# A rule for where the matmuls of two recurrences may enter a stream of projection matmuls

## The chip, the cores and the metric

The kernel runs on one core of a Trainium2 chip. The metric is the device time of one execution in microseconds (us), and the median of three runs before the change is 1229.77 us. TensorE runs the matmuls, VectorE (DVE) and ScalarE (ACT) the elementwise work, and SyncE (SP) issues most of the transfers.

## What is computed

One layer of a sequence model with 272 tokens (16 learned ones and 256 of the input) of width 2048. The tokens are normalised and multiplied by one wide weight matrix; its columns are the inputs of three recurrent mixers A, B and C, each with an output of width 1024. Each mixer's output is multiplied by a matrix of its own, gated and added, and a last matrix and a norm give the result.

```python
xn = rmsnorm(h, norm_g[l])
(a_q, a_f, a_i, a_z, b_q, ..., c_r, c_k, c_v, ..., g_a, g_b, g_c) = split_cols(xn @ w_in[l])
y_a = hgrn2_mixer(a_q, a_f, a_i, a_z, ...)      # A: 8 heads
y_b = mlstm_mixer(b_q, b_k, b_v, b_o, ...)      # B: 4 heads
y_c = rwkv7_mixer(c_r, c_k, c_v, c_wd, ...)     # C: 16 heads
merged = (sigmoid(g_a) * (y_a @ w_br[l, 0]) + sigmoid(g_b) * (y_b @ w_br[l, 1])
          + sigmoid(g_c) * (y_c @ w_br[l, 2]))
h = h + merged @ w_out[l]
```

Mixer A works in chunks: scores inside the chunk, weights from decays, a sum over values, a norm per head. Mixer B is a gated attention with a norm. Mixer C needs, for each chunk of 64 tokens, the inverse of a triangular matrix and then a chain of small products from chunk to chunk.

## The kernel before, in words

**The stream.** The big product is cut into projections of 256 columns (47 of them before the gates). One projection is `gemm` (line 390): four weight blocks `u` of four 128-row tiles, and for each block two column halves `j`. Weights and activations are split into a high and a low part of type fp32r, so each tile takes three matmuls; `unit` (line 377) issues the 12 matmuls of one half of a block, into the PSUM tile `gp`. A whole block is thus 24 matmuls. `Stream` brings the weights: `load` (line 343) issues the transfer on SyncE's queue, `cut` (line 351) makes `wh` on ScalarE and `wl` on VectorE, and `next` (line 367) keeps three cut blocks. A cut is emitted at the start of a block, for the block two further on.

**The recurrences.** `c_scan` (line 506), `b_scan` (line 965), `tail` of B's gates (line 875) and `a_scan` (line 1138) are Python generators that issue a few instructions and then yield. A yield of `"pe"` says that the next step begins with matmuls; another yield says that it doesn't. A scan starts with a priority: 0 for C, 1 for B, 2 for A. The four scans of A are called a0 to a3 here; each works on two heads and goes through these TensorE groups in turn: a first small group of 104 score matmuls (`aW`, `aQb`), a second small group of 72 (`aW`), a group of scores over longer distances (`aQR`), the transposes of the values (`aV`), the products with the values (`ATT`), and the column sum for the norm (`aYL`, `aYH`). B's heads go through `nM`, `bV` (twice), `bQ`, `bW` and the column sum `bHL`.

**The order.** The order of the program is made in Python by the class `Order` (line 44). It keeps a planned clock for TensorE, ScalarE and VectorE, adds an estimated cost for each instruction that is issued, and keeps for each scan the planned time at which its last result is ready. `pump` (line 87) goes over the scans in order of priority and lets each go on while its planned time is at most some distance ahead of TensorE's planned clock: 3.5 us for a step without matmuls, 0.3 us (2.0 us for C) for one with matmuls. `gemm` calls `pump` after each half of a block, so after 12 and after 24 matmuls. `finish` (line 105) issues all that is left of a scan at once; it is called where a later block needs the scan to be over. For A's scans that is behind the last projection of a group (until `ast["free"]` is set, line 1112) and behind the second projection of the next group (all of it, line 1122). Behind the program stands a scheduler that may still move an instruction that it holds to be unready behind later ones of its engine.

**Buffers.** The work tiles of A and B come from one set of six buffers (tag `wx`), and their PSUM banks from a pool of two (`bank`). C has sets of its own (`wc`, `cbank`).

Of the kernel before, what the change touches and what calls it, by code (L numbers as in the profile page):

```python
# [43 lines left out]
class Order:  # L44
# [39 lines left out]
            self.scans.remove(s)  # L84
        s["ready"], self.ready = self.ready, saved

    def pump(self):
        for e in ("act", "dve"):
            self.clk[e] = min(self.clk[e], self.clk["pe"] + self.CAP)
        moved = True  # L90
        while moved:
            moved = False
            for s in list(self.scans):
                while not s["done"]:
                    if s["hold"] is not None and not s["hold"]():
                        break
                    ahead = self.AHEAD
                    if s["pe"]:
                        ahead = self.AHEAD_PE if s["prio"] else self.AHEAD_PE_FIRST
                    if s["ready"] > self.clk["pe"] + ahead:  # L100
                        break
                    self.step(s)
                    moved = True
# [47 lines left out]
def kernel(  # L151
# [29 lines left out]
    od = Order()  # L181
# [195 lines left out]
    def unit(h, l, u, kts, ps, aH, aL, t0, n, js):  # L377
        for k in range(UK):
            kk = u * UK + k
            rh = aH[:, kk, t0:t0 + n]  # L380
            mm(ps, h[:, k, js], rh, start=kk == 0, stop=False)
            mm(ps, h[:, k, js], aL[:, kk, t0:t0 + n], start=False, stop=False)
            mm(ps, l[:, k, js], rh, start=False, stop=kk == kts - 1)

    def apart(f):
        saved, od.ready = od.ready, od.clk["pe"]
        f()
        od.ready = saved

    def gemm(m, aH, aL, kts, t0, n, evac):  # L390
        nt = m // P
        ps = [gps.tile([P, 512], F32, name="gp", tag="g") for _ in range(nt)]
        for u in range(kts // UK):
            h, l = ws.next()
            for j in range(nt):
                unit(h, l, u, kts, ps[j][:, 0:n], aH, aL, t0, n, slice(j * P, (j + 1) * P))
                od.pump()
        for j in range(nt):
            apart(lambda: evac(j, ps[j][:, 0:n]))

# [2 lines left out]
    def proj(c0, m, t0, evac, before=None, after=None):  # L403
        ws_src = win[:, :, c0:c0 + m]
        blocks.append((ws_src, KT, lambda: gemm(m, xH, xL, KT, t0, T - t0, evac), before, after))
# [1324 lines left out]
```

## Time and profile before

| | |
|---|---|
| Median of three runs | 1229.77 us (1229.72 to 1230.2) |
| The profiled execution: time | 1229.33 us |
| The profiled execution: span from the first to the last instruction | 1227.6 us |
| Mean granted TensorE clock | 0.998 |
| TensorE busy, VectorE busy, ScalarE busy | 98%, 72%, 54% of the span |

The time of an execution is its span and 1.7 us that lie around it. The profile comes from one execution, and its own time is 0.4 us below the median. A busy TensorE is not TensorE at its peak: its matmuls overlap, so the distance from one start to the next says more than the length of one.

### The profile page before, as it was taken

What the parts mean: (1) busy time and instruction counts of PE and PEld (TensorE: products, weight loads), DVE (VectorE), ACT (ScalarE), POOL (GpSimd) and SP (SyncE); (2) the same over time, 40 slices, a digit from 0 to 9 for tenths busy, and PEclk for the clock granted to TensorE, in tenths of its full rate; (3) what the DMA queues carried; (4) which work ended last, traced back from release to release, by engine and by line L of the source; (5) the groups of instructions that cost most, each with busy time, mean ns of one, the idle gap of its engine ahead of it and who ended that gap; (6) DMA issues with size and microseconds to landing.
All of it is one profiled execution on the core that took longest, in us unless ns stands there. A gap on an engine that the chain in (4) does not pass through costs nothing.

```text
span 1227.6 us, 23061 instructions
## 1 busy us (share of the span) xinstructions
PE 1208.1 (98%) x9224; PEld 1104.2 (90%) x9224; DVE 879.2 (72%) x1491; ACT 665.0 (54%) x1032; POOL 57.0 (5%) x167
## 2 busy tenths in 40 slices
PE   8999999999999999999999999999999999999997
PEld 8999999999999999999999988888888888888887
DVE  6688996697975889995889986644555565556554
ACT  6765455663445764766664657544444444445444
POOL 3100001000051000010000000000000000000000
PEclk9999999999999999999999999999999999999999
DMA  8645564465563554463554454666766676665663
GB/s 254 184 138 166 155 172 130 129 183 155 155 171 104 158 165 137 140 170 105 162 163 142 139 164 153 190 188 189 226 197 193 191 225 200 191 193 172 193 197 121
DMA packets 172996, 207.43 MB, mean 169 GB/s; under 512 B 22331, under 2 KB 127160, under 8 KB 172488
## 3 DMA queue, kind: packets, MB, share of 16 engines
q1 hardware_dynamic: 171688, 202.21, 56.2%
q0 software_dynamic: 880, 3.22, 0.8%
q8 instruction: 72, 1.18, 0.4%
q10 hardware_dynamic: 320, 0.53, 0.1%
q14 instruction: 36, 0.29, 0.1%
HBM read 202.19 MB, written 3.74 MB: 168 GB/s over the span
## 4 chain that ended last, share of the span: by engine, by line
PE 85%; DVE 9%; ACT 3%; issue 2%; POOL 0%; DVEq 0%; ACTq 0%; POOLq 0%
PE gp L186 76%; PE cbank L186 5%; DVE wl L127 3%; PE bank L186 3%; ACT wh L127 1%; DVE Ltmp L127 1%; PE cbank L193 1%; DVE LV L127 1%; PE bank L193 1%; DVE UV L127 0%; DVE aY L127 0%; ACT L127 0%; DVE BK L127 0%; DVE aW L127 0%; DVE SC L127 0%
## 5 line engine op out<-in xcount | busy, mean ns | idle before, releaser
L127 DVE TENSOR_TENSOR wl<-raw,wh 128x1024 fp32r<-128x1024 f32 (+1 forms) x370 | 449.3, 1215 | 243.6 <-ACT wh L127 242.2
L127 ACT CAST wh<-raw 128x1024 fp32r<-128x1024 f32 (+1 forms) x370 | 386.7, 1046 | 387.0 <-PE gp L186 352.4
L186 PE MATMUL gp<-xH,wh 128*128 128x272 f32 (+3 forms) x1552 | 448.1, 289 | 0.2 <-ACT xH L127 0.2
L186 PE MATMUL gp<-xH,wl 128*128 128x272 f32 (+3 forms) x1552 | 444.0, 286 | 1.6 <-DVE wl L127 1.6
L186 PE MATMUL gp<-xL,wh 128*128 128x272 f32 (+3 forms) x1552 | 443.8, 286 | 0.1
L186 PEld LDWEIGHTS gp<-xH,wl 128*128 128x128 f32 x1552 | 292.4, 188 | 2.9 <-DVE wl L127 2.6
L186 PEld LDWEIGHTS gp<-xH,wh 128*128 128x128 f32 x1552 | 292.5, 188 | 2.2 <-ACT xH L127 0.5
L186 PEld LDWEIGHTS gp<-xL,wh 128*128 128x128 f32 x1552 | 292.2, 188 | 0.9 <-DVE xL L127 0.3
L186 PE MATMUL gp<-wh,xH 128*128 128x512 f32 x384 | 150.6, 392 | 0.0
L186 PE MATMUL gp<-wh,xL 128*128 128x512 f32 x384 | 150.5, 392 | 0.0
L186 PE MATMUL gp<-wl,xH 128*128 128x512 f32 x384 | 150.3, 391 | 0.0
L186 PEld LDWEIGHTS gp<-wh,xL 128*128 128x128 f32 x384 | 72.1, 188 | 15.5
L186 PEld LDWEIGHTS gp<-wl,xH 128*128 128x128 f32 x384 | 72.2, 188 | 15.0
L186 PEld LDWEIGHTS gp<-wh,xH 128*128 128x128 f32 x384 | 72.1, 188 | 15.0
L186 PE MATMUL gp<-wh,mH 128*128 128x512 f32 (+1 forms) x144 | 51.1, 355 | 0.0
L186 PE MATMUL gp<-wh,mL 128*128 128x512 f32 (+1 forms) x144 | 50.9, 354 | 0.0
L186 PE MATMUL gp<-wl,mH 128*128 128x512 f32 (+1 forms) x144 | 50.9, 354 | 0.0
L127 DVE TENSOR_TENSOR LV<-LV,Ltmp 40x31 f32<-40x31 f32 (+15 forms) x124 | 41.0, 331 | 2.6
L127 DVE TENSOR_TENSOR Ltmp<-LU,LV 40x31 f32<-40x31 f32 (+15 forms) x124 | 41.1, 332 | 2.4
L186 PEld LDWEIGHTS gp<-wh,mL 128*128 128x128 f32 x144 | 27.2, 189 | 3.8
L186 PEld LDWEIGHTS gp<-wh,mH 128*128 128x128 f32 x144 | 27.2, 189 | 3.7
L186 PEld LDWEIGHTS gp<-wl,mH 128*128 128x128 f32 x144 | 27.2, 189 | 3.7
(420 smaller groups left out, 1476.0 us busy)
## 6 DMA issues: line engine op xcount, KB each, us to landing
raw<-in_w_in_dram SPq DMA_DIRECT2D x288, 512.0 KB, 3.7
raw<-in_w_br_dram SPq DMA_DIRECT2D x48, 512.0 KB, 4.2
raw<-in_w_out_dram SPq DMA_DIRECT2D x32, 512.0 KB, 3.6
hres<-in_x_dram POOLq DMA_DIRECT2D x2, 1024.0 KB, 5.9
xt<-in_x_dram SPq DMA_DIRECT2D x3, 512.0 KB, 5.0
raw<-in_w_in_dram SPq DMA_DIRECT2D x4, 256.0 KB
fg<-in_final_norm_g_dram POOLq DMA_DIRECT2D x1, 1024.0 KB, 5.1
scr<-SC SPq DMA_DIRECT2D x16, 40.0 KB, 1.7
```

What stands on the lines that cost most here:

```text
L127: r = f(*a, **k)
L186: nc.tensor.matmul(o, lhsT, rhs, start=start, stop=stop)
L193: nc.tensor.transpose(o, a, i)
```

## The change

`pump` gets an argument. Where it is false, a step that begins with matmuls, of a scan with a priority other than 0, is not let in. `gemm` passes false behind the first half of a weight block and true behind the second. The steps of A and B that begin with matmuls are therefore emitted behind whole blocks only, 24 matmuls apart instead of 12. C's steps, and the steps without matmuls of all three, are emitted as before, and so is everything in the later products, where `pump` is called without an argument. No instruction is added or taken away; only the order changes, and with it the planned clocks.

```diff
-    def pump(self):
+    def pump(self, whole=True):
+
         for e in ("act", "dve"):
             self.clk[e] = min(self.clk[e], self.clk["pe"] + self.CAP)
         moved = True
...
             for s in list(self.scans):
                 while not s["done"]:
                     if s["hold"] is not None and not s["hold"]():
+                        break
+                    if s["pe"] and s["prio"] and not whole:
                         break
                     ahead = self.AHEAD
...
             for j in range(nt):
                 unit(h, l, u, kts, ps[j][:, 0:n], aH, aL, t0, n, slice(j * P, (j + 1) * P))
-                od.pump()
+                od.pump(j == nt - 1)
```

## Rows read from the trace of the kernel before

**Rows 1.** The page: engines' busy time, VectorE's share and TensorE's clock in 40 slices.

```profile
PE 1208.1 (98%) x9224; PEld 1104.2 (90%) x9224; DVE 879.2 (72%) x1491; ACT 665.0 (54%) x1032; POOL 57.0 (5%) x167
...
DVE  6688996697975889995889986644555565556554
...
PEclk9999999999999999999999999999999999999999
```

**Rows 2.** The page: the chain that ended last, shares of the span by engine.

```profile
PE 85%; DVE 9%; ACT 3%; issue 2%; POOL 0%; DVEq 0%; ACTq 0%; POOLq 0%
```

**Rows 3.** Waits of TensorE: us in total, times, longest us.

```profile
PE bank L186 <- DVE aW L127: 1.6, 2, 1.0
PE gp L186 <- DVE wl L127: 1.6, 4, 0.7
...
PE bank L186 <- DVE aYL L127: 1.1, 2, 0.8
```

**Rows 4.** Timeline of TensorE (start us, us, instructions): first and last group behind half a block.

```profile
97.99 0.34 PE L193 MATMUL bank<-ident,gg 4*128 4x4 f32 x3
...
651.18 0.81 PE L186 MATMUL bank<-aW 128*32 128x32 f32 x67
```

**Rows 5.** Timeline of TensorE: a B group behind half a block, and the stream after.

```profile
186.81 0.97 PE L186 MATMUL bank<-bW,onesR 128*128 128x256 f32 x6
187.62 1.95 PE L186 MATMUL bank<-bW,bvt 128*128 128x256 f32 x12
189.42 0.36 PE L186 MATMUL gp<-xH,wh 128*128 128x258 f32 x1
```

**Rows 6.** Timeline of TensorE: the same group of another head, behind a whole block.

```profile
144.94 0.97 PE L186 MATMUL bank<-bW,onesR 128*128 128x256 f32 x6
...
147.56 0.37 PE L186 MATMUL gp<-xH,wh 128*128 128x272 f32 x1
```

**Rows 7.** Timelines of VectorE and TensorE: a last operand of B and its matmuls.

```profile
154.09 0.41 DVE L127 TENSOR_TENSOR bHL<-bSQ,bHL 128x256 fp32r<-128x256 f32 x1
...
158.23 0.40 PE L186 MATMUL bank<-bHL,onesR 128*128 128x256 f32 x2
```

**Rows 8.** Timeline of TensorE: the two small groups of a0 (in brackets: idle before, releaser).

```profile
473.43 0.81 PE L186 MATMUL bank<-aW 128*32 128x32 f32 x67
...
474.59 0.38 PE L186 MATMUL gp<-xH,wh 128*128 128x256 f32 x1
...
476.08 0.29 PE L186 MATMUL gp<-xH,wh 128*128 128x272 f32 x1
...
478.07 0.95 PE L186 MATMUL bank<-aW 128*32 128x32 f32 x72 [0.95 <-DVE aW L127]
```

**Rows 9.** Timeline of VectorE: a0's work between its two small groups.

```profile
474.95 0.43 DVE L127 TENSOR_TENSOR aW<-aE,aK 128x272 f32<-128x272 f32 x1
...
477.58 0.43 DVE L127 TENSOR_TENSOR aW<-aE,aQ 128x272 f32<-128x272 f32 x1
```

**Rows 10.** Timeline of TensorE: the end of a0.

```profile
499.74 0.82 PE L193 MATMUL bank<-ident,aV 128*128 128x128 f32 x6
...
503.53 0.37 PE L186 MATMUL gp<-xH,wh 128*128 128x256 f32 x1
...
506.89 0.36 PE L186 MATMUL bank<-aYL,onesR 128*128 128x256 f32 x1 [0.31 <-DVE aYL L127]
```

**Rows 11.** Timeline of VectorE: the last operand of that column sum.

```profile
506.07 0.68 DVE L127 TENSOR_TENSOR aYL<-aY,aYH 128x512 fp32r<-128x512 f32 x1
```

**Rows 12.** Stretches (length, busy us of each engine): while a0 and a2 run.

```profile
462.00:510.00 48.00, 46.74 (x553) 45.61 (x552) 46.37 (x109) 26.98 (x48) 0.32 (x2) 1.00 0.50 144
510.00:530.00 20.00, 19.35 (x158) 18.95 (x156) 19.79 (x43) 13.73 (x21) 0.00 (x0) 1.00 0.57 150
640.00:690.00 50.00, 48.52 (x570) 47.57 (x569) 46.94 (x109) 27.98 (x51) 0.13 (x1) 1.00 0.52 149
```

**Rows 13.** Timeline of VectorE: a1's work behind its first small group.

```profile
530.85 0.44 DVE L127 TENSOR_TENSOR aW<-aE,aK 128x272 f32<-128x272 f32 x1 [0.45 <-PE bank L186]
```

## Prediction

> **What bounds the kernel.** I read the page first. TensorE is busy for 98% of the span at full clock from end to end, and VectorE is uneven: nearly full in some slices, half idle in the last third [rows 1]. The chain that ended last is 85% TensorE and 9% VectorE [rows 2]. So time is won or lost only where TensorE stands or where its instructions lie further apart, and the second reading is the list of its waits. Most are short. Those that the change can touch directly are A's: 1.6 us in two waits for `aW`, 1.1 us in two for `aYL`, and with them 1.6 us in four waits of the stream itself for `wl`, the half of the weights that VectorE makes [rows 3]. They sum to 4.3 us, 0.35% of the time, and that bounds what a better order of A could bring.
>
> The third reading was the order of TensorE's matmuls around each group of A and B, counted in twelves of the stream. Of 44 places where such matmuls enter during the projections, 22 lie behind the first half of a block; the first is the group of B's gates at 97.99 us, the last a2's first small group at 651.18 us [rows 4]. Sixteen of these are B's and six A's. Those 22 have to move; the others already stand behind whole blocks, or were put a few matmuls further by the scheduler.
>
> **Does a place cost anything in itself?** The same B group, 18 matmuls, takes from 186.81 to 189.42 us behind half a block, 2.61 us, and from 144.94 to 147.56 us behind a whole one, 2.62 us [rows 5, 6]. So the move itself costs and gains 0: the matmuls are the same and the stream restarts alike. What is left is lateness: a moved group comes 12 matmuls later. In a0's projection these take from 474.59 to 476.08 us, 1.49 us [rows 8].
>
> **B's sixteen moves: 0.** B's operands are ready early. The tightest kind of step is the column sum: its operand ends at 154.50 us and its matmuls start at 158.23 us, 3.7 us later [rows 7]. B's order is set by the planned clock, not by data, and a delay of 1.49 us for each step leaves room before the next head's `finish`, or makes that `finish` issue elementwise work that TensorE needs only a block later. Cover: three cut weight blocks. Without it a B step could stand for at most the 1.49 us that it is late; that no wait for an operand of B is in the list at all speaks for 0. I take 0, with ends 0 and +1.5 us for one such miss.
>
> **A's first small group (a0 and a2 move; a1 and a3 already stand behind whole blocks): 0.** In a0 it runs at 473.43 us, and VectorE's next `aW` follows at 474.95 us; the last `aW` ends at 478.01 us and the second small group starts at 478.07 us after 0.95 us of standing [rows 8, 9]. VectorE's `aW` needs the buffers that the first group frees. So the chain first group, `aW`, second group is really a chain, and the move shifts it by up to 1.49 us. Does TensorE stand longer? The second group comes out of `finish`, and it stands a few matmuls inside the next block (which begins at 476.08 us), so the scheduler placed it by its own idea of when `aW` is ready. If the place goes along with the chain, the wait stays as it is; if the place stays, 1.49 us are added, twice (a0, a2), +3.0 us; if the place goes a whole half further, both waits vanish, -1.6 us [rows 3]. The place was made from the same chain, so I take 0 and keep -1.6 and +3.0 us.
>
> **A's later groups: +0.7 us.** Of a0, `aQR` and `aV` (499.74 us) stand behind halves and move. `ATT` comes one block after `aV` and ends where the stream goes on, at 503.53 us; the operand of the column sum `aYL` ends at 506.75 us, 3.2 us later, and TensorE stands 0.31 us for it behind the last matmul of that projection, where `finish` puts it [rows 10, 11]. With `aV` half a block later `ATT` can no longer be ready behind the third block and goes behind the fourth, the same place at which `finish` issues the column sum. Then nothing of the stream lies between them by program order, and what lies between them in the end is the scheduler's choice. If it puts enough of the stream between, the wait is 0: -0.3 us. If it puts nothing, 3.2 us instead of 0.31 us: +2.9 us. For a2, whose second group also comes later, the ends are -0.8 and +2.4 us. The scheduler's misses in the four A waits lie between 0.3 and 1.0 us [rows 3], so I take a miss near the upper end for both, 0.9 us against 0.31 and 0.81 us: +0.6 and +0.1 us, together +0.7 us (ends -1.1 and +5.3).
>
> **The stream's waits for `wl`: 0.** VectorE is busy for 46.4 of 48 us from 462 us, for 19.8 of the next 20, and for 46.9 of 50 us from 640 us [rows 12]. There it is close to being the bound, and four `wl` come late. What A no longer asks of VectorE at one moment, C's triangular inverse fills, and the sum of the work up to 530 us stays. A full engine finishes its queue at the same time in another order, unless it is made to stand. Bounds: all four waits gone, -1.6 us; or one half block more in each of the two stretches, +3.0 us. I take 0.
>
> In one place the trace shows VectorE standing for TensorE: 0.45 us before a1's `aW`, released by the first small group [rows 13]. By the Trainium skill ("TensorE: Matmul & The Clock Gate", section on the array of 32×32 sub-arrays) ScalarE and VectorE take their instructions strictly in order, so whatever waits at the head holds all behind it. Were that the whole story, the sum would be the rival below that holds VectorE's queue instead of 0.
>
> C's matmuls stay as they are, transfers keep their order on SyncE's queue (A and B issue none in the scans), GpSimd's few fills follow the same events.
>
> **Sum.** 0 + 0 + 0.7 + 0 = +0.7 us on the profiled execution of 1229.33 us (span 1227.6 us and 1.7 us around it) gives 1230.0 us; it lay 0.44 us below the median, so I forecast 1230.4 us for the median. What can be told from no change is about 0.2%, 2.5 us: the forecast is no measurable difference.
>
> **Rivals.**
> *Slower: the column sum stands right behind `ATT`.* As above, without the stream between: +2.9 us in a0 and +2.4 us in a2, 1235.1 us with both, 1232 to 1233 us with one or with half of each. It decides from the point at which fewer than about 12 stream matmuls lie between the two in both places. For it: `finish` issues them back to back. Against it: the scheduler has moved unready groups before, and a1's same groups show no wait.
> *Slower: VectorE's queue is held.* If `aW` of a0 and a2 stands at the head of VectorE's queue until the moved first group is done, VectorE stands up to 1.49 us in each, and as it is full until 530 us the next `wl` are as much later: +3.0 us, 1232.8 us. Against it: in a0 no such standing is seen today, since a `wl` and C's work lie in between; for it: the 0.45 us of a1 [rows 13].
> *Faster: A's waits dissolve.* If the later emission makes the scheduler put more of the stream ahead of the second small groups and the column sums, 2.7 us go; with the `wl` waits 4.3 us: 1225.5 to 1227.1 us. For it: these waits exist because the scheduler thought the operands ready too early. Against it: nothing in the change tells it better.
> *The change does not do what it says.* The scheduler behind the program may again put groups of A and B inside blocks, as it did twice with a0's and a2's second groups. Then the time is that of before, 1229.8 us.
>
> **Numbers.** The forecast gets 0.43, the rival without effect 0.10, the first slower one 0.20, the held queue 0.07, the faster one 0.20. Faster by over 0.2%: 0.20; within 0.2%: 0.53; slower: 0.27. The range leaves out the outer halves of the end cases: 1226.3 to 1234.2 us; the forecast's own range is 1228.2 to 1232.2 us.
>
> **What would show it.** Right: TensorE's groups of A and B only behind 24 matmuls (or further in, where `finish` issued them), each of the 18-matmul B groups still at 2.6 us, no new wait for an operand of B, a0's first small group near 474.7 us, `ATT` of a0 right behind the fourth block and the waits for `aYL` at most about 1 us each, waits for `wl` near 1.6 us in sum. Wrong: a wait for `aYL` or `aW` of 2 us or more; gaps of VectorE before `aW` released by TensorE's `bank`; waits of C's groups (`SC`, `UV`, `cX`) that grow although C was not touched, since the planned clocks that A and B advance are shared with it; or a total of A's and `wl`'s waits well under 2 us.

## The result, and the profile after

The changed kernel takes 1241.04 us (median of four runs, 1238.83 to 1241.42) against 1229.74 us (four runs, 1228.15 to 1230.20): a ratio of 1.0090, 95% interval 1.0073 to 1.0108. It is slower by 11.3 us, and the forecast of 1230.4 us, with its range up to 1234.2 us, is wrong. The profiled execution took 1240.92 us, its span is 1239.2 us and its mean granted clock 0.993, so 11.6 us of span are to be found. All lines have moved by three: the helper of the matmuls is L189 now, that of the transposes L196, that of the elementwise work L130.

The page of the changed kernel: engines, VectorE's share and TensorE's clock in 40 slices, and the chain by engine; these answer [rows 1, 2].

```profile
PE 1213.2 (98%) x9224; PEld 1108.1 (89%) x9224; DVE 877.8 (71%) x1491; ACT 665.3 (54%) x1032; POOL 50.4 (4%) x167
...
DVE  7687996697976889985879984744555565555554
...
PEclk9999999999999999999999998999999999999999
...
PE 83%; DVE 10%; ACT 3%; issue 2%; DMA 0%; SPq 0%; POOL 0%; DVEq 0%; ACTq 0%; POOLq 0%
```

The counts are the same. TensorE is idle for 26.0 us (1239.2 less 1213.2) against 19.5 us, and busy for 5.1 us more with the same matmuls; one slice of the clock, 743 to 774 us, has lost a tenth. Three stretches at half clock make up nearly all of these 5.1 us (last section).

Waits of TensorE in the changed kernel (us in total, times, longest us), against [rows 3]:

```profile
PE gp L189 <- DVE wl L130: 3.6, 3, 2.4
...
PE bank L189 <- DVE aQ L130: 1.5, 1, 1.5
PE bank L189 <- DVE aYL L130: 1.3, 2, 0.8
PE cbank L189 <- DVE cSL L130: 1.3, 1, 1.3
...
PE cbank L189 <- ACT UV L130: 1.1, 2, 1.0
...
PE bank L189 <- DVE aW L130: 1.1, 2, 0.6
PE cbank L189 <- ACT ZT L130: 1.1, 1, 1.1
```

The waits for `aW` and `aYL` have hardly changed. `wl` has one of 2.35 us, `aQ`, an operand of a2, has a new one, and `cSL`, `UV`, `ZT` are operands of mixer C, which the change doesn't touch. The best guide to the place is the start of the same matmul of the stream in both traces, worked out from the two timelines (after less before). The points are chosen where both kernels have issued equally many matmuls of the recurrences; only at 753.97 us has the changed kernel already issued 16 more of them:

| at (us, before) | 15 | 600 | 690 | 710 | 753.97: first product on mixer B's output | 1220 |
|---|---|---|---|---|---|---|
| later by (us) | -0.8 | -0.5 | +1.5 | +4.1 | +11.8 | +11.6 |

So the time goes at two places: 4.6 us between 600 and 710 us, ahead of the gates, and 7.7 us between 710 us and the first product on `yHB`, the high half of B's output. At the first place lie the wait for `aQ` and the long one for `wl`, which ends at 705.70 us, and the clock falls behind both (timeline of TensorE, after):

```profile
669.71 0.65 PE L189 MATMUL bank<-aQ,aK 128*64 128x64 f32 x8 [1.47 <-DVE aQ L130]
```

The second place lies between the product with the first 512 gate columns and the first product on `yHB`. There the changed kernel's TensorE does this (timeline):

```profile
755.08 0.40 PE L189 MATMUL gp<-wh,xL 128*128 128x512 f32 x1
755.57 0.45 PE L189 MATMUL cbank<-UV,BT 128*64 128x64 f32 x8
...
758.00 0.93 PE L189 MATMUL bank<-ATT,avt 128*128 128x256 f32 x4
...
761.37 0.29 PE L189 MATMUL cbank<-SC,UV 128*64 128x16 f32 x4 [0.97 <-ACT UV L130]
...
762.81 0.36 PE L189 MATMUL bank<-aYL,onesR 128*128 128x256 f32 x1 [0.79 <-DVE aYL L130]
...
764.78 0.55 PE L189 MATMUL cbank<-cSL,bonesR 128*128 128x256 f32 x1 [1.26 <-DVE cSL L130]
...
765.77 0.63 PE L189 MATMUL gp<-wh,yHB 128*128 128x512 f32 x1
766.20 0.63 PE L189 MATMUL gp<-wl,yHB 128*128 128x512 f32 x1
```

For 10.7 us the stream stands, and only the leftovers of C's last scan (`cbank`) and of a3 (`bank`) run. TensorE is busy for 7.33 us of them, the end of it at half clock, so less than 10.7 us is lost. In the kernel before the same groups of C lie between matmuls of the gate, and cost no waiting (its timeline):

```profile
741.15 0.39 PE L186 MATMUL gp<-wh,xL 128*128 128x512 f32 x1
741.47 0.45 PE L186 MATMUL cbank<-UV,BT 128*64 128x64 f32 x8
...
742.31 0.50 PE L186 MATMUL gp<-wh,xH 128*128 128x512 f32 x1
```

What ties the product to C can be read from the program and one row. `yHB` and `yLB` are allocated in `l_setup`'s pool, which takes the memory of C's pool when C's last scan is over, and ScalarE makes `yHB`. Before, and then after (tile `yHB`: ns shortest, median, longest; first and last start):

```profile
L127 ACT CAST yHB<-yB x4: 619/646/659, 746.9 to 756.5; 128x512 fp32r<-128x512 f32 x4
```

```profile
L130 ACT CAST yHB<-yB x4: 602/606/616, 764.3 to 767.7; 128x512 fp32r<-128x512 f32 x4
```

In both it follows the last small product of C's chain, which starts at 746.5 and at 761.7 us. Before it comes 0.4 us behind that, after 2.6 us, for there ScalarE first makes a last copy of C, C's squares and the gate. That chain waits for C's triangular inverse, 31 steps on VectorE, the last of which starts at 701.8 us before and at 719.1 us after (tile `LV`, before and after):

```profile
L127 DVE TENSOR_TENSOR LV<-LV,Ltmp x124: 171/350/419, 130.7 to 701.8; 40x31 f32<-40x31 f32 x8, 40x60 f32<-40x60 f32 x8, 40x87 f32<-40x87 f32 x8, 40x112 f32<-40x112 f32 x8
```

```profile
L130 DVE TENSOR_TENSOR LV<-LV,Ltmp x124: 174/350/418, 129.0 to 719.1; 40x31 f32<-40x31 f32 x8, 40x60 f32<-40x60 f32 x8, 40x87 f32<-40x87 f32 x8, 40x112 f32<-40x112 f32 x8
```

Why is the inverse 17 us late? The planner's own positions, in projections emitted before the step, name two causes. `second cV` is the step with the second transposes of C's values, the last one with matmuls ahead of the inverse; a2's `finish` stands behind 43 projections and issues a2 up to the point where its inputs are free:

```
             a1's tail ends   second cV   inverse: first step .. end
before           38.25         42.625        42.75  .. 45.75
after            38.75         43.125        43.125 .. 46.875
```

a1's later groups put its tail into the start of C's last scan (which begins behind projection 38): in the traces the first column sum of that scan runs at 601.3 us before and 603.7 us after, its scores `RA,BK` at 626.7 and 632.2 us. On the planned clock the step `second cV` went in at 736.3 us before; now it is planned ready at 749.0 us, and at the last look of `pump` ahead of a2's `finish` TensorE's planned clock is at 745.0 us: 4.0 us ahead, where 2.0 us are allowed. So the inverse is emitted behind what `finish` issues, and VectorE comes to it later: its fourth step of 31 starts at 644.3 us before and at 669.5 us after. This is theory 1. Its rivals were theory 2, that A's own late groups and the `wl` waits between 640 and 712 us are the cost, and theory 3, that B's sixteen moves are.

### The profile page after: what moved, and what is told of

Same layout as the page of the kernel before. It is cut to its first block, busy times and chain, and to the rows that moved or that the text cites. A ratio compares the mean times of both kernels' runs of the same rounds, so it can differ in the third digit from the quotient of the medians.

```text
span 1239.2 us, 23066 instructions
## 1 busy us (share of the span) xinstructions
PE 1213.2 (98%) x9224; PEld 1108.1 (89%) x9224; DVE 877.8 (71%) x1491; ACT 665.3 (54%) x1032; POOL 50.4 (4%) x167
## 4 chain that ended last, share of the span: by engine, by line
PE 83%; DVE 10%; ACT 3%; issue 2%; DMA 0%; SPq 0%; POOL 0%; DVEq 0%; ACTq 0%; POOLq 0%
PE gp L189 75%; PE cbank L189 5%; DVE wl L130 3%; PE bank L189 2%; ACT wh L130 1%; DVE Ltmp L130 1%; PE cbank L196 1%; DVE LV L130 1%; PE bank L196 1%; DVE UV L130 0%; DVE aE L130 0%; DVE aW L130 0%; DVE aM L130 0%; DVE BK L130 0%; DMA scv<-LV 0%
## 5 line engine op out<-in xcount | busy, mean ns | idle before, releaser
L130 DVE TENSOR_TENSOR wl<-raw,wh 128x1024 fp32r<-128x1024 f32 (+1 forms) x370 | 449.3, 1215 | 249.8 <-ACT wh L130 248.3
L130 ACT CAST wh<-raw 128x1024 fp32r<-128x1024 f32 (+1 forms) x370 | 386.4, 1046 | 401.4 <-PE gp L189 372.7
L189 PE MATMUL gp<-xH,wh 128*128 128x272 f32 (+3 forms) x1552 | 449.4, 290 | 0.2 <-ACT xH L130 0.2
L189 PE MATMUL gp<-xH,wl 128*128 128x272 f32 (+3 forms) x1552 | 445.5, 287 | 3.7 <-DVE wl L130 3.6
L189 PE MATMUL gp<-xL,wh 128*128 128x272 f32 (+3 forms) x1552 | 443.6, 286 | 0.1
L189 PEld LDWEIGHTS gp<-xH,wl 128*128 128x128 f32 x1552 | 293.7, 189 | 5.0 <-DVE wl L130 4.6
L189 PEld LDWEIGHTS gp<-xH,wh 128*128 128x128 f32 x1552 | 293.9, 189 | 2.6 <-ACT xH L130 0.5
L189 PEld LDWEIGHTS gp<-xL,wh 128*128 128x128 f32 x1552 | 293.6, 189 | 0.6 <-DVE xL L130 0.3
L189 PE MATMUL gp<-wh,xH 128*128 128x512 f32 x384 | 150.9, 393 | 0.0
L189 PE MATMUL gp<-wh,xL 128*128 128x512 f32 x384 | 150.3, 391 | 0.0
L189 PE MATMUL gp<-wl,xH 128*128 128x512 f32 x384 | 150.0, 390 | 0.0
L189 PEld LDWEIGHTS gp<-wh,xL 128*128 128x128 f32 x384 | 72.1, 188 | 15.7
L189 PEld LDWEIGHTS gp<-wh,xH 128*128 128x128 f32 x384 | 72.1, 188 | 15.1
L189 PEld LDWEIGHTS gp<-wl,xH 128*128 128x128 f32 x384 | 72.2, 188 | 15.0
L189 PE MATMUL gp<-wh,mH 128*128 128x512 f32 (+1 forms) x144 | 51.1, 355 | 0.0
L189 PE MATMUL gp<-wh,mL 128*128 128x512 f32 (+1 forms) x144 | 50.9, 354 | 0.0
L189 PE MATMUL gp<-wl,mH 128*128 128x512 f32 (+1 forms) x144 | 50.9, 354 | 0.0
L130 DVE TENSOR_TENSOR LV<-LV,Ltmp 40x31 f32<-40x31 f32 (+15 forms) x124 | 41.0, 331 | 2.5
L130 DVE TENSOR_TENSOR Ltmp<-LU,LV 40x31 f32<-40x31 f32 (+15 forms) x124 | 41.0, 331 | 2.4
L189 PEld LDWEIGHTS gp<-wh,mL 128*128 128x128 f32 x144 | 27.2, 189 | 3.8
L189 PEld LDWEIGHTS gp<-wh,mH 128*128 128x128 f32 x144 | 27.2, 189 | 3.7
L189 PEld LDWEIGHTS gp<-wl,mH 128*128 128x128 f32 x144 | 27.2, 189 | 3.7
```

Of the source, the lines that this page charges most:

```text
L130: r = f(*a, **k)
L189: nc.tensor.matmul(o, lhsT, rhs, start=start, stop=stop)
```

## The experiments

Times are medians; each ratio is to the kernel before in the same comparison (1229.2 to 1229.4 us in all of them).

**Whose groups?** The rule for B alone, for A alone, for all but a1, for a1 alone:

```diff
-                    if s["pe"] and s["prio"] and not whole:
+                    if s["pe"] and s["prio"] == 1 and not whole:                  # B alone; == 2: A alone
+                    if s["pe"] and s["prio"] and not whole and not s.get("free"): # all but a1
+                    if s["pe"] and s["prio"] and not whole and s.get("held"):     # a1 alone
...
             ast["scan"] = od.start(a_scan(g, st), 2)
+            ast["scan"]["free"] = g in (1,)      # or ["held"]
```

> The rule holds for B's scans alone; A's groups may enter behind halves as before. Theory 1 (a1's later tail puts off C's last scan, whose end the first gate product needs): a1's tail is where it was and C's last scan is planned to go into its triangular inverse ahead of a2's finish, as before, so 1229.8 us, 1228.5 to 1232, and the first matmul on yB starts within 2 us of the kernel before. Theory 2 (A's own late groups and the wl waits between 640 and 712 us cost it): 1229.8 us too. Theory 3 (B's sixteen moved groups cost it): 1236 us or more.

1228.99 us, ratio 0.9994 (0.9984 to 1.0004). Theory 3 falls.

> The rule holds for A's scans alone. Theory 1: C's last scan is again planned into its inverse only behind a2's finish, so nearly the whole loss, 1238 to 1241 us, with the first matmul on yB 9 us or more later than in the kernel before. Theory 2: the same time, but the loss lies ahead of the gates. Theory 3: 1230 us.

1238.93 us, 1.0084 (1.0067 to 1.0101). The stream stands for 10.7 us ahead of the first product, from 756.67 to 767.37 us, as in the changed kernel.

> The rule holds for B and for a0, a2 and a3, not for a1. Theory 1: a1's tail is planned 5 us earlier than in the changed kernel, C's last scan gets the values' second transposes in ahead of a2's finish but not the inverse, and its end is planned half way between both kernels: 1232 to 1237 us. Theory 2 (a2's own groups): 1240 us, as the changed kernel. Theory 3: 1240 us.

1235.22 us, 1.0047 (1.0030 to 1.0064), half the loss, as theory 1 had it from the planner. Here the wait is plain to see, since the leftovers don't fill it (timeline of TensorE):

```profile
755.33 0.72 PE L196 MATMUL bank<-ident,aV 128*128 128x128 f32 x4
758.29 0.50 PE L189 MATMUL gp<-wh,yHB 128*128 128x512 f32 x1 [2.24 <-ACT yHB L130]
```

> The rule holds for one of the four scans of A, a1, and for nothing else; of a1, the groups aQR, aV, ATT and aYL are what can move. Theory 1: that alone puts C's last scan behind a2's finish, 1237 to 1241 us, with TensorE nearly without the stream ahead of the first matmul on yB. Theory 2: a2's groups and a0's stand where they stood, so at most 1231.5 us. Theory 3: 1229.8 us.

1238.60 us, 1.0079 (1.0064 to 1.0094): one scan of four, of whose groups all but the first move (the second small group, too, from 536.60 to 538.53 us), brings four fifths of the loss. Theory 2 in its strong form, that a2's and a0's groups are needed, falls. But its trace has the late `wl`, too, waits of 2.2 and 2.1 us at 666 and 704 us, and so part of the loss is where theory 2 had it: from 600 to 710 us the stream loses 3.5 us here, 4.6 us with A alone, and nothing with all but a1.

**Is it the first product that pays?** Four kernels: the changed one with the gate branch's blocks in another order, that order in the kernel before, C's scan held in the kernel before, and C's scan let in earlier in the changed one.

```diff
+        if first:                                   # the first gate branch's blocks, in both kernels
+            G0, P0, G1, P1, G2, P2, G3, P3 = blocks[at:]
+            blocks[at:] = [G0, G1, P0, G2, P1, G3, P2, P3]
```

> The changed kernel with the blocks of the first gate branch in another order: gate, gate, product, gate, product, gate, product, product instead of gate and product by turns. C's last scan stays as late as in the changed kernel. Theory 1 (the first product on yB waits for C's last scan, whose memory yHB and yLB take): the second gate's 20 us of stream cover the wait, and the time is 1230 us, 1228 to 1232.5, though the first cast to yHB is still 10 us or more later than in the kernel before. Rival (C's leftover groups hold TensorE themselves, each waiting for the one before, whatever the stream has to do): 1238 us or more.

> The same order of the first gate branch in the kernel before. Theory 1: there is little to cover, since C's last scan ends with the first gate's stream; 1229.5 us, 1227 to 1231. Rival (the other order is worth something by itself, so what it gives the changed kernel says nothing of the wait): 1224 us or less.

1232.99 us, 1.0038 (1.0025 to 1.0051), and 1229.45 us, 1.0001 (0.9992 to 1.0010). The order is worth nothing by itself, and takes 7.7 of the 11.3 us from the changed kernel, though the last product of C's chain is still at 758.5 us and the first cast at 761.4 us. The time is 0.5 us above the upper end of what was expected. C's groups now lie between the second gate's matmuls, and the wait for `UV` is gone (timeline of TensorE):

```profile
757.84 0.40 PE L189 MATMUL gp<-wh,xL 128*128 128x512 f32 x1
758.17 0.29 PE L189 MATMUL cbank<-SC,UV 128*64 128x16 f32 x4
...
758.75 0.50 PE L189 MATMUL gp<-wh,xH 128*128 128x512 f32 x1
```

Not all of the gain comes from the stand, though. At 710 us this kernel is 1.7 us later than the kernel before, and the changed kernel 4.1 us: the waits for `aQ` and `wl` are nearly as long in both (1.48 and 2.18 us here), but here the clock doesn't fall behind them. Behind 710 us it loses 1.4 us, and the changed kernel 7.5 us. What is left is waiting, not the product: TensorE is busy for 1208.0 us of 1230.7, so idle for 22.7 us against 19.5, and the 3.2 us more are the 3.1 us of span. Two of the waits lie ahead of the gates, one in the first gate: 2.18 us for `wl` at 704.78 us, 1.48 us for `aQ` at 670.24 us, 1.09 us for `ZT` at 731.41 us, against 0.73 and 0.23 us for `wl` and 0.81 us for `aYL` that the kernel before has in that stretch.

```diff
+        if g == 3:                                   # kernel before: ahead of the second cV step
+            yield lambda: od.halves >= 345           # halves of blocks emitted
```

> The kernel before, without the rule; only C's last scan is held ahead of the second transposes of its values until the first half of the 44th projection's first block is out, which is where the changed kernel's plan has that step; the last step of its inverse is then planned behind 46.9 projections, as in the changed kernel, against 45.8. Theory 1: that lateness alone costs as much as the change, 1238 us, 1235 to 1241, and TensorE goes nearly without the stream ahead of the first product on yB. Rival (a1's later tail costs by itself, through VectorE or through the order of A's groups): at most 1232 us.

1234.52 us, 1.0046 (1.0034 to 1.0059): slower without the rule and with a1 where it was, but below 1235 us, the lower end of what was expected. C's scan starts on time here and only its inverse lies behind a2's `finish`: the last step is at 711.9 us, 10.1 us late instead of 17.3 us. The stream stands from 752.95 to 757.67 us ahead of the first product (timeline of TensorE):

```profile
752.95 0.39 PE L188 MATMUL gp<-wh,xL 128*128 128x512 f32 x1
...
757.02 0.36 PE L188 MATMUL cbank<-cSL,bonesR 128*128 128x256 f32 x1 [2.30 <-DVE cSL L129]
...
757.67 0.63 PE L188 MATMUL gp<-wh,yHB 128*128 128x512 f32 x1
```

So either cause makes C late, and the changed kernel has both. C's lateness by itself costs 5.2 us here, most of it at the second place: at 690 us, with equally many matmuls issued, this kernel is only 1.2 us later than the kernel before.

```diff
-                        ahead = self.AHEAD_PE if s["prio"] else self.AHEAD_PE_FIRST
+                        ahead = self.AHEAD_PE if s["prio"] else s.get("lead", self.AHEAD_PE_FIRST)
...
+            if g == 3:
+                st["scan"]["lead"] = 8.0             # 4.0 in the next two
```

> The changed kernel, with the steps of C's last scan that begin with matmuls let in when they are planned ready up to 8 us ahead of TensorE's clock instead of 2 us. By the plan the second transposes then go in behind 41.75 projections instead of 43.1, and the inverse ends behind 45.25 instead of 46.9; A and B keep the rule. Theory 1: 1229 us, 1227 to 1233 (some waits of C's groups may come in, for they are let in sooner than they are ready). Rival (A's and VectorE's own delays ahead of the gates): 1238 us or more.

> As the kernel that lets C's last scan in up to 8 us ahead, but with 4 us: by the plan the second transposes go in behind 42.1 projections and the inverse ends behind 45.6, which is closest to the kernel before (42.6 and 45.75). A and B keep the rule. If the lateness of C's last scan is what the change costs, and the 8 us only brought in a waiting group of C with a fall of the clock at 630 us, then 1230.5 us, 1229 to 1232.5. If letting C in early by any amount costs as much as it saves: 1233 us or more.

> The kernel before, without the rule, with C's last scan let in up to 4 us ahead of TensorE's planned clock. With the rule this lead left 2.9 us of the loss. If that rest belongs to the rule (A's groups late): 1229.3 us here, 1228 to 1230.8. If it is the price of the lead itself (C's groups come before they are ready, and its work pushes A's and the weight blocks): 1231.5 us or more here too.

With 8 us 1233.53 us, 1.0038 (1.0024 to 1.0052), 0.5 us above the upper end of what was expected; with 4 us 1232.04 us, 1.0022 (1.0013 to 1.0032); with 4 us in the kernel before 1231.19 us, 1.0017 (1.0008 to 1.0026), between the two forecasts. With the rule on and C brought forward, the stand ahead of the first product is gone (0.2 us with 8 us of lead, 0.8 us with 4, and 0.8 us in the kernel before). But the lead has a price of its own: 2.0 us in the kernel before, which leaves some 0.9 us of the 2.9 us to the rule if the price is the same with it. With 8 us it shows as a stretch at half clock behind groups that came too early (granted clock, last column but two; this profiled execution took 1236.25 us, 2.7 us more than the median):

```profile
632.00:638.00 6.00, 6.00 (x26) 5.68 (x27) 2.95 (x7) 1.80 (x3) 0.00 (x0) 0.50 0.33 54
```

**Can the product start without C?** The changed kernel with `yHB` in the two `wups` and the low half in `WDH` and `WDL`, tiles that C's last scan reads last at its start, and with the split emitted ahead of C's last `finish`. Half of the low half is left out: four slices are made and each is used twice.

```diff
+                st["h"] = Pieces(lambda k: up4[k // 4][:, k % 4, :])     # up4: the two wups
+                st["l"] = Pieces(lambda k: low4[k % 4][:, 0:SEQ])        # low4: WDH + WDL
...
                 if first and jb == 0:
+                    split()
                     l_setup()
```

> The changed kernel with the two halves of yB in memory that C's last scan doesn't use late, split ahead of the first gate and ahead of C's last finish in the program. Only half of the low half is made, and used twice; the matmuls are as many as before. C's last scan is as late as in the changed kernel. If the first product waited for C's memory and for its place behind C on ScalarE, the product's matmuls start within 1 us of the end of the gate's stream, C's leftovers lie between them, and the time is 1233 us, 1231.5 to 1235, as with the gates ahead. If TensorE was held by the leftover groups themselves: 1239 us or more.

1237.01 us, 1.0071 (1.0056 to 1.0085), 2 us above the upper end of what was expected. The place does what theory 1 says: the casts run long before, from 245.1 to 600.2 us, and the product starts as the gate ends, with C's chain between its matmuls (timeline of TensorE; the operands are named after the tiles that now hold them):

```profile
753.36 0.40 PE L189 MATMUL gp<-wh,xL 128*128 128x512 f32 x1
753.85 0.45 PE L189 MATMUL cbank<-UV,BT 128*64 128x64 f32 x8
...
754.70 0.50 PE L189 MATMUL gp<-wh,wups 128*128 128x512 f32 x1
755.04 0.40 PE L189 MATMUL gp<-wl,wups 128*128 128x512 f32 x1
755.27 0.40 PE L189 MATMUL gp<-wh,WDH 128*128 128x512 f32 x1
755.63 0.71 PE L189 MATMUL cbank<-UV,SC 128*128 128x128 f32 x4
```

Against the kernel before, the first product is 0.7 us late, the gate that follows 4.0 us, and the end 7.0 us. The last 3 us grow slowly, in the products alone: the matmuls on `yHC` whose weights are `wl` start 233.3 ns behind the one before them instead of 227.0 ns (mean of 64), at a granted clock of 1.00 in both kernels. What this edit changed for them is where the tiles lie in memory; that this is the reason was not tested. It is a difference that the changed kernel doesn't have. As the edit moved the split in memory and in program order together, it doesn't tell which of the two held the product.

**Is there anything else in it?**

> The rule holds for B and for a0 and a3; a1 and a2 are let in behind halves as before. By the plan C's last scan is then exactly where it is in the kernel before (inverse begins behind 42.75 and ends behind 45.75 projections). If the change costs only through C's last scan: 1229.3 us, 1228 to 1230.8. If some 3 us of the cost are A's own groups and the weight blocks behind them, whatever C does: 1231.5 us or more.

(The `free` of above, for `g in (1, 2)`.) 1228.72 us, 0.9996 (0.9987 to 1.0005). With the rule for B, a0 and a3, and C's plan as it was, nothing is left of the loss. This was open after the kernels with the remedies, and it settles it: the whole loss comes by a1 and a2. What of it they cost through C, and what by their own lateness, this kernel doesn't tell.

> The rule for a2 alone. By the plan that is enough to put the inverse of C's last scan behind a2's finish (43.125 instead of 42.75; it ends behind 46.4), with a1's tail where it was. If the lateness of C's last scan is the cost, 1234.5 us, 1232.5 to 1237, near the kernel with a1 exempt (1235.2 us), with a wait or a thin stretch ahead of the first product. If a2 costs through its own waits alone: at most 1231 us and no thin stretch there.

(The `held` of above, for `g in (2,)`.) 1233.28 us, 1.0030 (1.0018 to 1.0041): a2 alone makes C late, too. By the plan all but the first step of the inverse is behind a2's `finish`; in the trace the steps run nearly as in the kernel before up to 693 us, and the last four come late, the last of them at 706.0 us. The last product of C's chain is at 754.5 us. The place of the payment was wrong: there is no stand ahead of the first product, but one inside C's chain, with a clock at 0.58 from 728 to 732 us behind it:

```profile
727.24 0.71 PE L189 MATMUL cbank<-Vm,ZT 32*32 32x32 f32 x32 [2.74 <-ACT ZT L130]
```

> The kernel before, with A's steps that begin with matmuls let in when they are planned ready up to 2 us ahead of TensorE's clock instead of 0.3 us: the opposite of the change. By the plan a1's tail ends behind 37.0 projections instead of 38.25, and C's inverse behind 45.6 instead of 45.75. If an earlier tail of A helps C's last scan further, it is worth little, since the gate's first product doesn't stand in the kernel before: 1229.5 us, 1227.5 to 1232, with new waits for A's operands against what comes earlier. If A's lateness costs by itself everywhere: 1226 us or less.

```diff
+                        ahead = (self.AHEAD_PE_FIRST, self.AHEAD_PE, 2.0)[s["prio"]]      # kernel before
```

1234.79 us, 1.0043 (1.0031 to 1.0055); expected was no change. The opposite of the change is slower as well: A's groups come early and wait (1.3 us for `aQ`), C's inverse ends at 707.0 us, 5.2 us later than in the kernel before although the plan has it earlier, and the first product's blocks wait 1.5 us for `yLB`. No version beat the kernel before; the ones that equal it are those in which C's last scan is left where it was.

C's last scan in the kernels, by their traces (us) and the planner (projections); the kernel with the split moved has no cast to `yHB`, and the kernel before with the gates ahead is as the kernel before:

| kernel | planned end of inverse | a1's column sum | last step of inverse | last product of C's chain | first cast to `yHB` | time |
|---|---|---|---|---|---|---|
| before | 45.75 | 586.9 | 701.8 | 746.5 | 746.9 | 1229.7 |
| B alone | 45.75 | 585.7 | 700.6 | 745.0 | 745.4 | 1229.0 |
| all but a1, a2 | 45.75 | 586.1 | 701.1 | 745.6 | 746.1 | 1228.7 |
| a2 alone | 46.4 | 586.9 | 706.0 | 754.5 | 754.9 | 1233.3 |
| all but a1 | 46.4 | 586.4 | 705.6 | 751.5 | 757.6 | 1235.2 |
| before, C held | 46.9 | 587.0 | 711.9 | 753.6 | 756.5 | 1234.5 |
| a1 alone | 46.9 | 589.2 | 717.9 | 760.4 | 763.0 | 1238.6 |
| A alone | 46.9 | 591.0 | 720.8 | 763.3 | 765.9 | 1238.9 |
| after | 46.9 | 589.2 | 719.1 | 761.7 | 764.3 | 1241.0 |
| after, gates ahead | 46.9 | 589.7 | 716.7 | 758.5 | 761.4 | 1233.0 |
| after, C 8 us ahead | 45.25 | 590.5 | 702.1 | 746.4 | 748.7 | 1233.5 |
| after, C 4 us ahead | 45.6 | 589.7 | 696.1 | 744.0 | 744.4 | 1232.0 |
| before, C 4 us ahead | 45.6 | 586.1 | 700.1 | 747.8 | 748.2 | 1231.2 |
| before, A 2 us ahead | 45.6 | 570.9 | 707.0 | 750.8 | 754.0 | 1234.8 |

In the nine rows down to "after" the time goes with C, though not step by step: with the inverse on time it is 1228.7 to 1229.7 us, with the inverse 4 to 10 us late 1233.3 to 1235.2 us, and with the inverse 16 to 19 us late 1238.6 to 1241.0 us. The three rows with C let in early show that C on time is not enough: their inverse ends at 702.1 us or sooner, and they take 2.0 to 4.2 us more than the kernel before. With all but a1 the cast comes 6.1 us behind the last product; from 751.87 us up to it ScalarE is busy with copies to `ATT`, C's squares and the gate. So there ScalarE's order holds the split as well.

## Why the prediction was wrong

**The step that failed** is "C's matmuls stay as they are". It costs no term of the sum, and it carried the result. The text itself named, as what would show it wrong, "waits of C's groups (`SC`, `UV`, `cX`) that grow although C was not touched, since the planned clocks that A and B advance are shared with it": that is what came, and it had neither a price nor a chance. In its place the runs show that C's last inverse ends 17.3 us later and that the stream stands for 10.7 us ahead of the first product; C held back in the kernel before, without the rule, costs 5.2 us (1234.52 us). The working looked at each moved group for the wait in front of that group. What a later group pushes was followed only to the next group of the same scan, while the planner carries it on to any scan that is issued after it, and C's last scan has a deadline, the first product on B's output, a hundred microseconds further. A misreading helped: "In one place the trace shows VectorE standing for TensorE" [rows 13] holds for `aW` alone. Such waits are largest in sum for C's operands, 14.6 us for `cX` and 9.1 us for `UV`: C's chain goes to and fro between the two engines (waits of VectorE, before):

```profile
DVE cX L127 <- PE cbank L186: 14.6, 13, 2.5
```

**The second miss** lies in the step "A's later groups: +0.7 us". It priced a0 and a2, where waits stood, and took a1's calm ("a1's same groups show no wait") for safety. But of the six moves of A that the text counted two are a1's, its second small group at 536.60 us and the transposes of its values at 576.85 us; neither has a term. What lies behind them moves too: its scores over longer distances run at 572.66 instead of 570.28 us, its column sum at 589.2 instead of 586.9 us. They are the ones that meet C's start. a2's cost through C, 4.1 us alone, wasn't seen either.

**The third miss** is the clock. The text read it as full from end to end [rows 1] and priced waits alone. The three falls of the clock, worked out in the last section at some 5 us, are the 5.1 us by which TensorE is busy for longer in the trace; each stands behind waits, though not every such wait brings one.

**What came out as forecast.** The move itself and B's sixteen moves cost 0: 0.9994 for B alone. A's first small groups cost 0: a0's runs at 473.55 us, 12 matmuls later in a trace whose stream is 1.3 us earlier there, and the second waits 0.63 us instead of 0.95. `ATT` of a0 did go behind the fourth block, as the text said, and the wait for `aYL` grew from 0.31 us [rows 10] to 0.55 us, within the end of 1 us (the changed kernel's timeline):

```profile
503.52 0.84 PE L189 MATMUL bank<-ATT,avt 128*128 128x256 f32 x4
...
508.17 0.36 PE L189 MATMUL bank<-aYL,onesR 128*128 128x256 f32 x1 [0.55 <-DVE aYL L130]
```

So the first slower rival did not happen, nor did the second: there is no longer wait for `aW`, and with a1 and a2 exempt but a0 under the rule the time is that of before. The faster rival did not happen either: the waits for `aW` and `aYL` are 2.4 us in sum, against 2.7 us.

**The `wl` waits: 0, with +3.0 us as the end.** They came to 3.6 us from 1.6. "What A no longer asks of VectorE at one moment, C's triangular inverse fills" was the reason for 0; it is right for the sum of the work and wrong for the deadline. At 704 us the late inverse, a2's tail and a3's start share VectorE, and the weights come behind them (timelines of VectorE and of TensorE, after):

```profile
703.15 0.34 DVE L130 TENSOR_TENSOR LV<-LV,Ltmp 40x192 f32<-40x192 f32 x1
...
703.77 0.74 DVE L130 TENSOR_TENSOR aE<-aC 128x256 f32<-128x256 f32 x2
704.44 1.21 DVE L130 TENSOR_TENSOR wl<-raw,wh 128x1024 fp32r<-128x1024 f32 x1
```

```profile
705.70 0.58 PE L189 MATMUL gp<-xH,wl 128*128 128x256 f32 x1 [2.35 <-DVE wl L130]
```

In the kernel before the same weights are made at 700.17 us, ahead of a3's start, and the inverse has one short step left, at 701.8 us; after, seven steps are still to come. How much of the wait is the inverse's and how much is the place of a3's start was not separated.

**The sum as the runs give it:** 7.7 us of the 11.3 us go when the second gate covers the stand ahead of the first product; of the 8.5 us between the two traces 6.1 us lie behind 710 us, and 2.4 us ahead of it, where the same waits stand but the clock doesn't fall. The other 3.6 us are waits, for `aQ` and `wl` ahead of the gates and for `ZT` in the first gate. All of it vanishes when a1 and a2 keep their places. Two things stay open: what makes the operands late at the first place, C's inverse on VectorE or a1's and a2's own groups, and how much of the tie between the split and C's end is memory and how much ScalarE's order.

## What to carry to other kernels

Where one planner serves several recurrences, a rule for some of them is a change to all: follow the planned clocks to the next thing with a deadline, and print the planned places before and after: here they tell in a few lines that C's last scan moves. They are no forecast of the time, for A let in 2 us ahead has the inverse planned earlier and loses 5.6 us. Look for the step that takes over memory at the end of a phase, and ask how late its last tenant may be; here the first cast runs 7 us ahead of the product that needs it, and a tenant 10 to 17 us later used that up. Here A let in later and A let in earlier both lose. Putting independent work ahead of the deadline (a second gate block) is a cheap insurance: it gives back 7.7 us where C is late, and costs and brings nothing where nothing is (1.0001).

## What the hardware showed that was not expected

Three times in the changed kernel TensorE's clock falls to the half level, 1.2 GHz, and stays there while TensorE is full again; in the same part of the kernel before it doesn't (length, then PE, PEld, DVE, ACT, POOL; the granted clock is the last column but two):

```profile
671.29:674.60 3.31, 3.31 (x18) 3.31 (x17) 3.28 (x7) 1.30 (x3) 0.00 (x0) 0.52 0.73 181
705.60:709.20 3.60, 3.50 (x17) 3.50 (x18) 3.60 (x11) 0.00 (x0) 0.00 (x0) 0.53 0.59 156
765.70:770.40 4.70, 4.70 (x13) 3.71 (x12) 3.26 (x5) 2.85 (x5) 0.57 (x1) 0.50 0.01 3
755.10:765.70 10.60, 7.33 (x76) 6.15 (x75) 4.62 (x10) 8.16 (x20) 1.46 (x2) 0.90 0.17 49
```

Ahead of the first fall TensorE stood for 1.47 us, ahead of the second for 2.35 us; ahead of the third it was busy for 7.33 of 10.6 us, with 76 matmuls and three waits of 0.8 to 1.3 us among them. In the kernel with the gates ahead it stood for 1.48 and 2.18 us at the first two places, and the clock stayed at 1.00 (the same columns, behind the 1.48 us):

```profile
671.00:676.00 5.00, 5.00 (x41) 4.88 (x42) 4.88 (x12) 2.87 (x10) 0.00 (x0) 1.00 0.65 191
```

With a1 alone it stood for 2.21 us at 666 us without a fall, and for 2.13 us at 704 us with one. So the length of the wait does not tell here whether the clock falls behind it. At the half level the product's matmuls follow each other at 427 ns (765.77, 766.20 and so on). The Trainium skill ("TensorE: Matmul & The Clock Gate", section "Wait — 56ns, not 53.3ns?") gives 426.7 ns for 512 columns at that level, and the trace agrees.

What the falls cost is an estimate from spacings at either level. The first: 15 spacings from 671.42 to 674.81 us, 3.39 us, which at 0.126 us would take 1.89 us, so 1.5 us. The second: 14 spacings from 705.70 to 708.86 us, 3.16 us, which at the 0.118 us of the matmuls behind them would take 1.65 us, so 1.5 us. The third: the first ten spacings of the product take 4.27 us, and at the 0.233 us of the full clock 2.33 us, so 1.9 us. Together they come to 4.9 us, against the 5.1 us by which TensorE is busy for longer.
